# Inverse Fourier products in plain float32 in place of three products of split operands

## Chip, cores and metric

The kernel runs on one core of a Trainium2 chip. Its time is the device time of one execution in microseconds; the median of several executions counts.

## What is computed

One inference step of a two-layer backbone: a Hyena layer (a long convolution by Fourier transforms) and a layer of multi-head latent attention, for 1024 sample tokens and 128 prompt tokens of 1024 channels. The change touches the long convolution of the first layer alone:

```python
def hyena_mix(h, w_in, conv_w, conv_b, ..., f_bias, w_out):
    n = 2 * L
    proj = h @ w_in
    u = short_conv(proj[..., :3 * HY_WIDTH], conv_w, conv_b)
    gate = proj[..., 3 * HY_WIDTH:]
    x0, x1, v = jnp.split(u, 3, axis=-1)
    z = (v * x1).astype(jnp.float32)
    hf = jnp.fft.rfft(filt, n=n, axis=0)
    hf = hf[:, :HY_WIDTH] + jnp.conj(hf[:, HY_WIDTH:])
    y = jnp.fft.irfft(jnp.fft.rfft(z, n=n, axis=1) * hf, n=n, axis=1)[:, :L]
    y = (y + z * f_bias.astype(jnp.float32)).astype(h.dtype) * x0
    return (y * jax.nn.silu(gate)) @ w_out
```

## The kernel before

The channels are worked in eight groups of 128. In the first stage a group's input projections, filter and forward transform are made (`hyena_group`), and the product of spectra goes to DRAM: `PS` for the sample (eight blocks of frequencies, real and imaginary, 128 x 128 each), `PP` for the prompt. The stage that the change touches comes next, from about 600 us on. In it `inverse` (line 532 on) makes y of a group: it loads the spectra in four pairs of blocks (`pi_raw`), multiplies them on TensorE by constant matrices (`ic`, 3200 columns; for the prompt `ip`, 256 columns), evicts the PSUM tile `iv_ps` by ScalarE into `Z` (the first pair) or `W` (the others), line 553, and combines these by 21 operations of VectorE (`ds`, `bf`, `yv`, lines 99 and 102). For five of the groups GpSimd multiplies y by the gate `xg` (`gate_y`, line 99), and y is stored in `YD`, to be loaded again when its place in SBUF is free.

A float32 matrix product is made of three products in float32r, a format that TensorE reads in one go: operand x is split into `hi`, x rounded to float32r, and `lo`, the exact rest, and hi·hi + hi·lo + lo·hi are summed in PSUM. For the spectra ScalarE makes hi (`pi_h`) and GpSimd lo (`pi_l`), for the prompt's (`pp_h`, `pp_l`) ScalarE and VectorE. The constants are split when the stage begins (`load_const`): 13 pieces of 256 columns pass through two buffers `cst`, ScalarE makes hi and VectorE lo.

Beside the inverse transforms TensorE makes the input projections that are left (`in_proj`, line 415: `ip_ps`, 384 columns each, 72 a projection), for x0 and the gate of the last groups; their weights are split by ScalarE and GpSimd (`wi_h`, `wi_l`). The list `PLAN` says how both alternate, `i` being an inverse without `gate_y`. A scheduler orders each engine's instructions when the program is built, and each engine then takes its own in that order; all loads and stores of this stage stand in SP's queue, in order too. Tiles share their places in SBUF: a tile waits until the users of what lay there are done.

Behind the stage `w_out` (line 627, `wo_ps`) needs y of all groups, split again (`lhh`, `lhl`), and then comes the attention layer.

Of the kernel before, what the change touches and what calls it, by code (L numbers as in the profile page):

```python
# [17 lines left out]
P = 128  # L18
D = 1024
# channel groups whose x0 and gate are made along with a group's forward transform  # L20
GATES = (0, None, None, 1, None, None, None, None)
NY = 6          # channel groups inverted before the input projection ends
# [20 lines left out]
# the steps of a unit of attention (scores of the next one, transposes, products with the values)  # L43
# [10 lines left out]
NT = 9          # token tiles: 8 of the sample, 1 of the prompt  # L54
# [15 lines left out]
# columns of the per-partition vector table  # L70
NK = 1408       # keys: 1024 of the sample, 256 of the cache, 128 of the prompt
# [4 lines left out]
class K:  # L76
# [8 lines left out]
    # hi = x rounded to float32r, lo = the exact rest  # L85
# [18 lines left out]
    # ---------------------------------------------------------------- adaLN  # L104
    def ada_chunk(self, layer, o, n, pool, ps, kk, bufs):
        """n columns from o of silu(cond) @ ada_w, as four partial sums on rows 32g + cond."""
# [12 lines left out]
    def ada_col(self, layer, m, o, n, pool, ps, kk, bufs):  # L119
        """columns o.. of shift and scale with the channel on the partition."""  # L120
        self.ada_turn(layer, m, o, n, self.ada_chunk(layer, o, n, pool, ps, kk, bufs), ps)
# [10 lines left out]
    def ada_mod(self, layer, m, A, k):  # L132
        """A = norm_w (1 + scale) for the channel tiles k."""
        c = C_NORM + 8 * layer
        nw = self.cols[:, c + k.start:c + k.stop].unsqueeze(2).broadcast_to([P, k.stop - k.start, 2])
        self.stt(A[:, k], m[:, 8 + k.start:8 + k.stop, :], 1.0, nw, ALU.mult, ALU.add)

    def ada_row(self, layer, gd, o, n, pool, ps, kk, bufs):
        """columns o.. of the gates as rows in DRAM."""
# [13 lines left out]
    # ------------------------------------------------- RMSNorm and modulate  # L153
# [11 lines left out]
    def norm(self, xs, ys, pool, eng=None):  # L165
        """ys = rmsnorm(xs) without its weight; the squares pass through ys, or a tile of their own."""
# [17 lines left out]
    def norm_mod(self, xs, tiles, pool, ps, A, B, hT, lT):  # L184
        """h^T (hi, lo): [128 channels, 8, tokens] of rmsnorm(x) * A + B, for neighbouring token tiles."""
# [12 lines left out]
    def modulate(self, x, k, c, pool, A, B):  # L198
        """x^T A + B for the channels k of the third c of the tokens."""
# [10 lines left out]
    # ------------------------------------------------------------- filters  # L210
    def sin_layer(self, pool, ps, w, src, kk, out, col):
        """out = sin(freq * (w^T src + b)) with the argument reduced to [-pi, pi]."""
# [14 lines left out]
    def load_w3(self, pool, g, bufs):  # L227
        """the last filter weights of 128 channels, forward and backward, on both halves of the rows."""
# [6 lines left out]
    def filters(self, pool, ps, hs):  # L235
        """hs: hidden features [hi; lo] by token."""
# [16 lines left out]
    # -------------------------------------------------------- long convolution  # L253
    def group_filter(self, g, q):
        """time-domain filter of 128 channels into the filter columns of E and O, and of the prompt."""
# [10 lines left out]
        # forward and backward taps: the sample at 0, the prompt at 1025, a zero behind each  # L266
# [9 lines left out]
        # the taps over the sums of their absolute values  # L276
# [11 lines left out]
        # sum and difference of the forward taps and the reversed backward ones  # L288
# [55 lines left out]
    def dft_tile(self, k0, ab, q):  # L344
        """the frequencies k0 + 16 m of z (columns 0:128) and of the filter (128:256)."""
# [22 lines left out]
    def product(self, pt, special, q, out):  # L368
        """out [128, 2, 128] = z * filter; special: row 0 holds two real frequencies."""
# [18 lines left out]
    # ------------------------------------------------------------ Hyena: in  # L388
# [15 lines left out]
    def in_proj(self, m, q, cb):  # L404
        """128 output channels of h @ hy_w_in; cb(psum, token offset)."""
# [16 lines left out]
    def conv_in(self, m, q):  # L422
        """one of x0, x1, v: projection, then the short convolution; [128, 1153] with column 1024 unused."""
        q["last"] = self.in_proj(m, q, lambda pt, o: self.conv_cb(pt, o, q))
        return self.conv(m, q)
# [19 lines left out]
    def hyena_group(self, g, q):  # L445
# [21 lines left out]
        # sample  # L467
# [7 lines left out]
        # prompt  # L475
# [54 lines left out]
    # ----------------------------------------------------------- Hyena: out  # L530
    def inverse(self, g, q):
        """y = irfft(product): [128 channels, T]."""
        nc, pool, ps = self.nc, q["pool"], q["ps"]
        ih, il, jh, jl = q["ih"], q["il"], q["jh"], q["jl"]
        # blocks 1 2 3 7 6 5 of (real, imaginary), and the blocks 0 (even, odd) and 4
        W = pool.tile([P, 6, 2, P], F32, name="W", bufs=1)
        Z = pool.tile([P, 2, 2, P], F32, name="Z", bufs=1)
        for ks, dst in (((0, 4), Z), ((1, 7), W[:, 0:4:3]), ((2, 6), W[:, 1:5:3]), ((3, 5), W[:, 2:6:3])):
            pt = ps.tile([P, 2, 256], F32, name="iv_ps", tag="iv_ps", bufs=3)
            raw = pool.tile([P, 2, 2, P], F32, name="pi_raw", bufs=4)  # L540
            h = pool.tile([P, 2, 2, P], F32R, name="pi_h", bufs=3)
            l = pool.tile([P, 2, 2, P], F32R, name="pi_l", bufs=3)
            st = ks[1] - ks[0]
            nc.sync.dma_start(raw, q["PS"][g][:, ks[0]:ks[1] + 1:st])
            self.hi("act", h, raw)
            self.lo("pool", l, raw, h)
            for b, k0 in enumerate(ks):
                for ri in range(2):
                    o = 256 * ri if k0 == 0 else 512 + 384 * (k0 - 1) + P * (1 - ri)
                    for s, (x, w) in enumerate(((h, ih), (h, il), (l, ih))):  # L550
                        self.PE.matmul(pt[:, b, :], x[:, b, ri, :], w[:, o:o + 256],
                                       start=ri == 0 and s == 0, stop=ri == 1 and s == 2)
# [5 lines left out]
        # d: W1 - W7, W2 - W6, W3 - W5 in blocks 0, 2, 4 (imaginary: 1, 3, 5), s: the sums in blocks 6..11  # L558
# [10 lines left out]
        # a0 a3 a2 a1 in blocks 0..3  # L569
# [22 lines left out]
        # prompt  # L592
        pt = ps.tile([P, 2, 256], F32, name="iv_ps", tag="iv_ps", bufs=3)
        raw, h, l = (pool.tile([P, 2, P], t, name=n, bufs=1) for n, t in (("pp_raw", F32), ("pp_h", F32R), ("pp_l", F32R)))
        nc.sync.dma_start(raw, q["PP"][g])
        self.hi("act", h, raw)
        self.lo("dve", l, raw, h)
        for ri in range(2):
            for s_, (x, wt) in enumerate(((h, jh), (h, jl), (l, jh))):
                self.PE.matmul(pt[:, 0, 0:P], x[:, ri, :], wt[:, P * ri:P * ri + P],  # L600
                               start=ri == 0 and s_ == 0, stop=ri == 1 and s_ == 2)
# [8 lines left out]
    def load_w(self, src, pool, ncol, tag, bufs, raw_bufs=2, hi_eng="act", lo_eng="dve", lo_bufs=None, step=2, tag_raw="w_raw", size=None, stage=None):  # L610
        """a [128, kt, ncol] weight chunk, split."""
# [17 lines left out]
    # ------------------------------------------------------------------ run  # L629
# [25 lines left out]
    def hyena(self):  # L655
# [9 lines left out]
        # in thirds of the tokens: the first ones' place comes free before the last product ends  # L665
# [12 lines left out]
        with self.pool("hsp", side="right") as hp:  # L678
            hs = hp.tile([P, T], F32R, name="hs")
            q.update(hs=hs)  # L680
            with self.pool("fp", 2, side="right") as fp, self.pool("ap", side="right") as ap, \
# [6 lines left out]
                # the normed tokens with the channel on the partition: in places of the convolution's and of x  # L688
# [14 lines left out]
                # the first two projections, along the channels as they come  # L703
# [5 lines left out]
                # shift and scale of 256 channels at a time; a chunk is turned after the next one's products  # L709
# [28 lines left out]
            with self.pool("pf", side="right") as fpool, self.pool("pa", 2, side="right") as pool, \  # L738
                    self.pool("pas", space=PSUM) as ps:
                # what only the filters need lies first: its place is the first to come free  # L740
# [22 lines left out]
        # the constants take the place of what only the filters needed  # L763
        with self.pool("pc", side="right") as pc, self.pool("pb1", 1, side="right") as pool, \
                self.pool("pb1s", space=PSUM) as ps:
            with self.urgent():
                ih, il = self.load_const(pc, "ic", 512 + 7 * 384, pc, "cst", 256, nc.sync)
                jh, jl = self.load_const(pool, "ip", 256, pc, "cst", 256, nc.sync)
            q.update(pool=pool, ps=ps, ih=ih, il=il, jh=jh, jl=jl)
# [15 lines left out]
        # once more in place of the constants: the weights of w_out and y  # L785
# [711 lines left out]
```

## Time and profile before

| | |
|---|---|
| median of 3 executions | 1869.53 us (1867.89 to 1870.08) |
| profiled execution | span 1868.4 us; its own time beside the span isn't recorded |
| TensorE busy | 1785.4 us (96%), 11480 matmuls |
| VectorE busy | 1291.5 us (69%) |
| ScalarE busy | 1116.4 us (60%) |
| GpSimd busy | 616.9 us (33%) |
| chain that ended last | TensorE 51%, VectorE 5%, DMA 2% of the span |

The span runs from the first to the last instruction. In the profile PE is TensorE's matmuls, PEld its loads of weights, DVE VectorE, ACT ScalarE, POOL GpSimd, SP the engine that issues transfers. A matmul's recorded duration contains its way through the array; the pace of a row of matmuls is read from their starts. A plain float32 product is recorded as two matmuls.

### The profile page before, as it was taken

The page shows a single profiled execution, that of the slowest core. Times are in us where ns is not written, and L with a number is a line of the kernel's source. Part 1 is how long each engine was busy: PE and PEld are TensorE (multiplying, and loading weights), DVE is VectorE, ACT ScalarE, POOL GpSimd, SP SyncE. Part 2 cuts the span into 40 slices and gives each one's busy share as a digit, 9 for nine tenths or more (in the row PEclk, how much of TensorE's full clock was granted, in tenths as well). Part 3 has the DMA queues.
Part 4 walks back from the last instruction along what each step waited for, and adds up shares of the span by engine and source line. Part 5 has one row for each costly group of instructions (what it writes and reads, how often), then busy time and mean ns, then how long its engine had stood idle before and what let it go on. Part 6 is the DMA issues. An engine that isn't in the chain of part 4 may idle for free.

```text
span 1868.4 us, 31762 instructions
## 1 busy us (share of the span) xinstructions
PE 1785.4 (96%) x11480; PEld 1585.0 (85%) x11480; DVE 1291.5 (69%) x2556; ACT 1116.4 (60%) x2650; POOL 616.9 (33%) x796
## 2 busy tenths in 40 slices
PE   6998999999999977999999989999999999999998
PEld 4887888887888877788999979999899998998786
DVE  3847887888865699753233268877887888778454
ACT  7655566665653443434353368878887888788431
POOL 2334433344345574233000042424343342235100
PEclk9999999999999988999999989999999999999999
DMA  8222232222223553731313410101010000012541
GB/s 316 83 84 72 66 94 93 82 82 66 74 95 112 168 167 103 279 134 65 94 33 109 102 31 19 42 16 46 20 37 28 20 28 24 18 35 62 180 134 68
DMA packets 126500, 157.93 MB, mean 85 GB/s; under 512 B 12711, under 2 KB 99687, under 8 KB 125064
## 3 DMA queue, kind: packets, MB, share of 16 engines
q1 hardware_dynamic: 123280, 152.51, 25.3%
q10 hardware_dynamic: 2552, 3.39, 0.6%
q8 instruction: 90, 1.47, 0.3%
q14 instruction: 66, 0.54, 0.1%
q0 software_dynamic: 512, 0.02, 0.0%
HBM read 113.89 MB, written 36.73 MB: 81 GB/s over the span
## 4 chain that ended last, share of the span: by engine, by line
PE 51%; DVE 5%; DMA 2%; ACT 1%; SPq 1%; issue 1%; POOL 0%; DVEq 0%; ACTq 0%; POOLq 0%
PE wo_ps L627 18%; PE wo_ps L1289 11%; PE av_ps L1174 8%; PE nm_ps L1162 7%; PE wo_ps L991 4%; PE nm_ps L1023 1%; DVE mx L1292 1%; DVE bf L99 1%; DMA og_in<-og 1%; SPq L978 1%; DMA y<-YD 0%; DVE kT L96 0%; PE nm_ps L842 0%; DMA wm_raw<-wm_a 0%; DVE yv L102 0%
## 5 line engine op out<-in xcount | busy, mean ns | idle before, releaser
L1289 PE MATMUL wo_ps<-kT,qT 128*128 128x512 f32 (+1 forms) x1152 | 281.4, 375 | 11.0 <-POOL qT L90 6.5
L1296 ACT ACTIVATE prob<-wo_ps,mx 128x512 f32<-128x512 f32 (+1 forms) x384 | 234.1, 618 | 22.9 <-DVE mx L1294 20.8
L1292 DVE TENSOR_REDUCE mx<-wo_ps 128x1 f32<-128x512 f32 (+1 forms) x384 | 213.0, 596 | 32.8 <-PE wo_ps L1289 32.1
L88 ACT ACTIVATE pt_h<-nm_ps 128x512 fp32r<-128x512 f32 x324 | 192.8, 599 | 70.4 <-PE nm_ps L1162 62.4
L1289 PEld LDWEIGHTS wo_ps<-kT,qT 128*128 128x128 f32 x1152 | 189.1, 191 | 46.4 <-ACT prob L1296 14.5
L96 DVE TENSOR_TENSOR pt_l<-nm_ps,pt_h 128x512 fp32r<-128x512 f32 x324 | 210.6, 683 | 13.0 <-ACT pt_h L88 12.8
L1162 PE MATMUL nm_ps<-ident,prob 128*128 128x128 f32 x1280 | 191.5, 272 | 0.0
L96 POOL TENSOR_TENSOR wi_l<-wi_raw,wi_h 128x512 fp32r<-128x512 f32 x64 | 127.3, 1989 | 185.1 <-ACT wi_h L88 181.7
L1162 PEld LDWEIGHTS nm_ps<-ident,prob 128*128 128x128 f32 x1280 | 150.0, 140 | 8.5
L415 PE MATMUL ip_ps<-lT,wi_h 128*128 128x384 f32 x720 | 157.1, 346 | 0.0
L415 PE MATMUL ip_ps<-hT,wi_l 128*128 128x384 f32 x720 | 152.8, 344 | 0.0
L415 PE MATMUL ip_ps<-hT,wi_h 128*128 128x384 f32 x720 | 152.5, 346 | 0.0
L1174 PE MATMUL av_ps<-pt_h,Vt 128*128 128x256 f32 x640 | 138.1, 297 | 0.0
L1174 PE MATMUL av_ps<-pt_l,Vt 128*128 128x256 f32 x640 | 135.4, 293 | 0.4 <-DVE pt_l L96 0.4
L415 PEld LDWEIGHTS ip_ps<-lT,wi_h 128*128 128x128 f32 x720 | 128.3, 192 | 6.7 <-issue 4.4
L415 PEld LDWEIGHTS ip_ps<-hT,wi_h 128*128 128x128 f32 x720 | 126.0, 190 | 6.4 <-issue 4.4
L415 PEld LDWEIGHTS ip_ps<-hT,wi_l 128*128 128x128 f32 x720 | 125.2, 189 | 7.1 <-issue 4.7
L627 PE MATMUL wo_ps<-wm_h,lhh 128*128 128x256 f32 (+1 forms) x432 | 126.5, 296 | 2.3 <-ACT wm_h L88 2.2
L1186 POOL TENSOR_SCALAR gt<-gt,sm 128x64 f32<-128x64 f32 x128 | 54.9, 443 | 220.6 <-DVE sm L1177 219.3
L627 PE MATMUL wo_ps<-wm_l,lhh 128*128 128x256 f32 (+1 forms) x432 | 127.1, 295 | 0.0
L627 PE MATMUL wo_ps<-wm_h,lhl 128*128 128x256 f32 (+1 forms) x432 | 126.7, 295 | 0.0
L99 POOL TENSOR_TENSOR pr<-ev 128x256 f32<-128x256 f32 x72 | 79.2, 1102 | 129.9 <-ACT ev L372 78.7
(354 smaller groups left out, 4348.2 us busy)
## 6 DMA issues: line engine op xcount, KB each, us to landing
wi_raw<-w_in SPq DMA_DIRECT2D x64, 256.0 KB, 3.0
ada_w<-ada_w SPq DMA_DIRECT2D x64, 256.0 KB, 2.8
x_in<-xs SPq DMA_DIRECT2D x16, 512.0 KB, 5.3
ada_w<-ada_w SPq DMA_DIRECT2D x8, 1024.0 KB
PS<-pr_o SPq DMA_DIRECT2D x64, 128.0 KB, 2.5
pi_raw<-PS SPq DMA_DIRECT2D x32, 256.0 KB, 3.6
YD<-yv SPq DMA_DIRECT2D x8, 576.0 KB, 4.5
y<-YD SPq DMA_DIRECT2D x8, 576.0 KB
```

The lines of the kernel that those rows point to most:

```text
L88: self.S.activation(out, src, AF.Copy)
L96: e.tensor_tensor(out, src, hi.bitcast(F32), ALU.subtract)
L99: (eng or self.V).tensor_tensor(out, x, y, op)
L415: mm = self.PE.matmul(pt, w[:, k, :], x[c][:, k, :], start=s == 0 and k == 0, stop=s == 2 and k == 7)
L627: self.PE.matmul(pt, x[k][:, sl], w[:, k, :], start=s == 0 and k == 0, stop=s == 2 and k == kt - 1)
L991: self.PE.matmul(pt[:, :n], x[:, k, o:o + P], y[:, k, c], start=s == 0 and k == 0, stop=s == 2 and k == kt - 1)
L1162: self.PE.transpose(pt[:, P * i:P * i + P], u["p"][i % 2][n // 2][:, P * (2 * (n % 2) + i // 2):P * (2 * (n % 2) + i // 2) + P], self.ident)
L1174: self.PE.matmul(u["po"][:, :256], m["V"][:, 2 * n + e, j, :], u[n][1 + s][:, 256 * e:256 * e + 256], start=n == first and e + s == 0, sto ...
L1186: self.G.tensor_scalar(o, o, u["sm"][:, i, 3:4], None, ALU.mult)
L1289: self.PE.matmul(pt[:, :n], x[:, j, P * i:P * i + P], y[:, j, o:o + n], start=s == 0, stop=s == 2)
L1292: self.V.tensor_reduce(mx[:, b:b + 1], c["s", i, b][:, :n], AX.X, ALU.max)
L1296: self.S.activation(c["p"][i][b], c["s", i, b][:, :n], AF.Exp, bias=c["mx"][i][:, 3:4], accum_out=c["sm"][:, i, b:b + 1])
```

## The change

The splits of the inverse transforms' operands go. The constants are loaded as they are, `ic` in two pieces and `ip` in one; spectra and constants are multiplied as float32. `W`, `Z` and `pp_raw` get second buffers. In `inverse`:

```diff
-        ih, il, jh, jl = q["ih"], q["il"], q["jh"], q["jl"]
-        W = pool.tile([P, 6, 2, P], F32, name="W", bufs=1)
-        Z = pool.tile([P, 2, 2, P], F32, name="Z", bufs=1)
+        ic, ip = q["ic"], q["ip"]
+        W = pool.tile([P, 6, 2, P], F32, name="W", bufs=2)
+        Z = pool.tile([P, 2, 2, P], F32, name="Z", bufs=2)
...
             raw = pool.tile([P, 2, 2, P], F32, name="pi_raw", bufs=4)
-            h = pool.tile([P, 2, 2, P], F32R, name="pi_h", bufs=3)
-            l = pool.tile([P, 2, 2, P], F32R, name="pi_l", bufs=3)
...
-            self.hi("act", h, raw)
-            self.lo("pool", l, raw, h)
...
-                    for s, (x, w) in enumerate(((h, ih), (h, il), (l, ih))):
-                        self.PE.matmul(pt[:, b, :], x[:, b, ri, :], w[:, o:o + 256],
-                                       start=ri == 0 and s == 0, stop=ri == 1 and s == 2)
+                    self.PE.matmul(pt[:, b, :], raw[:, b, ri, :], ic[:, o:o + 256], start=ri == 0, stop=ri == 1)
...
-        raw, h, l = (pool.tile([P, 2, P], t, name=n, bufs=1) for n, t in (("pp_raw", F32), ("pp_h", F32R), ("pp_l", F32R)))
+        raw = pool.tile([P, 2, P], F32, name="pp_raw", bufs=2)
         nc.sync.dma_start(raw, q["PP"][g])
-        self.hi("act", h, raw)
-        self.lo("dve", l, raw, h)
...
-            for s_, (x, wt) in enumerate(((h, jh), (h, jl), (l, jh))):
-                self.PE.matmul(pt[:, 0, 0:P], x[:, ri, :], wt[:, P * ri:P * ri + P],
-                               start=ri == 0 and s_ == 0, stop=ri == 1 and s_ == 2)
+            self.PE.matmul(pt[:, 0, 0:P], raw[:, ri, :], ip[:, P * ri:P * ri + P], start=ri == 0, stop=ri == 1)
```

and where the stage begins:

```diff
-                ih, il = self.load_const(pc, "ic", 512 + 7 * 384, pc, "cst", 256, nc.sync)
-                jh, jl = self.load_const(pool, "ip", 256, pc, "cst", 256, nc.sync)
+                ic = pc.tile([P, 512 + 7 * 384], F32, name="ic", bufs=1)
+                nc.sync.dma_start(ic[:, 0:1664], a["ic"][:, 0:1664])
+                nc.sync.dma_start(ic[:, 1664:], a["ic"][:, 1664:])
+                ip = pc.tile([P, 256], F32, name="ip", bufs=1)
+                nc.sync.dma_start(ip, a["ip"])
```

The scheduler makes another order of the stage; before and behind it the order is the same. On TensorE, where the inverse products begin, before (iv_ps are the inverse products, ip_ps the projections; rows are equal instructions in a row):

```order
L415 MATMUL ip_ps<-hT_121,wi_h 128x384 x7
L551 MATMUL iv_ps<-ic_h,pi_h 128x256
L551 MATMUL iv_ps<-ic_l,pi_h 128x256
L415 MATMUL ip_ps<-hT_121,wi_h 128x384
L415 MATMUL ip_ps<-lT_122,wi_h 128x384 x5
L551 MATMUL iv_ps<-ic_h,pi_l 128x256
L551 MATMUL iv_ps<-ic_h,pi_h 128x256
L551 MATMUL iv_ps<-ic_l,pi_h 128x256
L551 MATMUL iv_ps<-ic_h,pi_l 128x256
L415 MATMUL ip_ps<-lT_122,wi_h 128x384 x3
L415 MATMUL ip_ps<-hT_121,wi_l 128x384 x4
```

and now (line 546 is the inverse product of the sample, 591 that of the prompt):

```order
L415 MATMUL ip_ps<-hT_121,wi_l 128x384 x8
L415 MATMUL ip_ps<-hT_123,wi_h 128x384 x3
L546 MATMUL iv_ps<-ic,pi_raw 128x256 x12
L415 MATMUL ip_ps<-hT_123,wi_h 128x384 x5
L415 MATMUL ip_ps<-lT_124,wi_h 128x384
L546 MATMUL iv_ps<-ic,pi_raw 128x256 x4
L591 MATMUL iv_ps<-ip,pp_raw 128x128 x2
L415 MATMUL ip_ps<-lT_124,wi_h 128x384 x5
L546 MATMUL iv_ps<-ic,pi_raw 128x256 x4
L415 MATMUL ip_ps<-lT_124,wi_h 128x384 x2
L415 MATMUL ip_ps<-hT_123,wi_l 128x384 x6
L546 MATMUL iv_ps<-ic,pi_raw 128x256 x12
```

The inverse products begin 20 projections later (108 behind the last product of adaLN, 88 before) and stand closer: 112 projections among them in place of 231, and 221 behind them in place of 122. On GpSimd, in the middle of the stage, before:

```order
L99 TENSOR_TENSOR yv<-yv,xg 128x1152
L96 TENSOR_TENSOR pi_l<-pi_raw,pi_h 128x512 x5
L99 TENSOR_TENSOR yv<-yv,xg 128x1152
L96 TENSOR_TENSOR pi_l<-pi_raw,pi_h 128x512 x3
L96 TENSOR_TENSOR wi_l<-wi_raw,wi_h 128x512
L99 TENSOR_TENSOR yv<-yv,xg 128x1152
L96 TENSOR_TENSOR pi_l<-pi_raw,pi_h 128x512 x2
```

and now, from the second weights of a projection to the end of the stage:

```order
L96 TENSOR_TENSOR wi_l<-wi_raw,wi_h 128x512 x3
L99 TENSOR_TENSOR yv<-yv,xg 128x1152 x2
L99 TENSOR_TENSOR cv<-cv 128x1024
L99 TENSOR_TENSOR cv<-cv 128x128
L96 TENSOR_TENSOR wi_l<-wi_raw,wi_h 128x512
L99 TENSOR_TENSOR yv<-yv,xg 128x1152
L96 TENSOR_TENSOR wi_l<-wi_raw,wi_h 128x512
L99 TENSOR_TENSOR yv<-yv,xg 128x1152 x2
L96 TENSOR_TENSOR wi_l<-wi_raw,wi_h 128x512 x4
```

The 32 splits of spectra are gone; the gate products of y, one of x0 with its gate (`cv`) and the weights' splits are left.

## Rows read from the trace of the kernel before

**Rows 1.** The page, part 2: busy tenths in 40 slices of 46.7 us

```profile
PE   6998999999999977999999989999999999999998
DVE  3847887888865699753233268877887888778454
```

**Rows 2.** Windows: us, busy PE, PEld, DVE, ACT, POOL, PEclk, DMA share, GB/s

```profile
611.70:763.40 151.70, 126.48 (x787) 122.97 (x786) 135.03 (x200) 58.72 (x123) 79.23 (x46) 0.91 0.46 147
640.00:740.00 100.00, 75.38 (x469) 73.05 (x469) 99.24 (x144) 35.34 (x74) 60.71 (x35) 0.86 0.43 135
```

**Rows 3.** Waits, 600 to 760: us in total, times, longest us

```profile
ACT Z L553 <- DVE bf L99: 32.4, 6, 7.0
PE iv_ps L551 <- ACT Z L553: 13.4, 5, 4.4
```

**Rows 4.** Windows: one group on VectorE without, one with GpSimd at work

```profile
744.96:753.07 8.11, 8.11 (x49) 8.11 (x48) 8.04 (x22) 2.38 (x4) 0.00 (x0) 1.00 0.18 73
719.61:735.55 15.94, 11.32 (x68) 11.12 (x68) 15.87 (x25) 5.42 (x11) 8.10 (x6) 0.89 0.21 75
```

**Rows 5.** Timeline of VectorE: start, us, engine, line, operation, count

```profile
725.67 1.84 DVE L99 TENSOR_TENSOR yv<-bf,ds 128x256 f32<-128x256 f32 x2
...
734.12 1.43 DVE L99 TENSOR_TENSOR cv<-cv 128x1024 f32<-128x1024 f32 x2
...
748.36 0.76 DVE L99 TENSOR_TENSOR yv<-bf,ds 128x256 f32<-128x256 f32 x2
```

**Rows 6.** Timeline of GpSimd beside the first of them

```profile
725.57 1.32 POOL L96 TENSOR_TENSOR wi_l<-wi_raw,wi_h 128x512 fp32r<-128x512 f32 x1 [0.17 <-ACT wi_h L88]
```

**Rows 7.** Groups, 600 to 760: busy us, mean ns | idle before, releaser

```profile
L96 POOL TENSOR_TENSOR pi_l<-pi_raw,pi_h 128x512 fp32r<-128x512 f32 x32 | 46.1, 1456 | 16.0 <-ACT pi_h L88 11.2 <-PE iv_ps L600 2.5 <-DMA pi_raw<-PS 2.1
...
L96 DVE TENSOR_TENSOR ic_l<-cst,ic_h 128x256 fp32r<-128x256 f32 x12 | 8.2, 698 | 15.8 <-ACT ic_h L88 15.8
...
L96 DVE TENSOR_TENSOR pp_l<-pp_raw,pp_h 128x256 fp32r<-128x256 f32 x8 | 5.5, 690 | 0.0
```

**Rows 8.** Line 99 on GpSimd, 600 to 760: ns min/median/max, first and last start

```profile
L99 POOL TENSOR_TENSOR yv<-yv,xg x5: 2619/2690/7564, 649.8 to 716.7; 128x1152 f32<-128x1152 f32 x5
L99 POOL TENSOR_TENSOR cv<-cv x4: 457/1424/2391, 598.3 to 632.1; 128x1024 f32<-128x1024 f32 x2, 128x128 f32<-128x128 f32 x2
```

**Rows 9.** Timeline of TensorE

```profile
644.39 0.22 PE L600 MATMUL iv_ps<-ip_h,pp_h 128*128 128x128 f32 x1
...
645.01 0.33 PE L551 MATMUL iv_ps<-ic_h,pi_h 128*128 128x256 f32 x1
...
646.49 2.26 PE L415 MATMUL ip_ps<-hT,wi_l 128*128 128x384 f32 x12
648.59 0.28 PE L551 MATMUL iv_ps<-ic_h,pi_h 128*128 128x256 f32 x1
...
649.90 0.28 PE L551 MATMUL iv_ps<-ic_h,pi_l 128*128 128x256 f32 x1
```

**Rows 10.** Windows: the lowest clock of the stage

```profile
670.00:680.00 10.00, 5.43 (x27) 5.10 (x26) 9.93 (x10) 5.20 (x11) 9.66 (x5) 0.58 0.58 185
```

**Rows 11.** Timeline of TensorE, plain float32: the first recorded matmul, then both

```profile
38.13 0.64 PE L215 MATMUL sf_ps<-zt,w 33*64 33x512 f32 x1
38.13 1.07 PE L215 MATMUL sf_ps<-zt,w 33*64 33x512 f32 x2
```

**Rows 12.** SP's queue at the stage's start, and a window with the loads under way

```profile
602.78 0.94 SPq L516 DMA_DIRECT2D cst<-ic  x2
...
608.00:612.00 4.00, 4.00 (x26) 4.00 (x25) 0.44 (x1) 2.79 (x7) 2.75 (x3) 1.00 0.99 324
```

**Rows 13.** Timeline of TensorE at the end of the projections, and a window

```profile
761.97 1.55 PE L415 MATMUL ip_ps<-hT,wi_h 128*128 128x384 f32 x8
764.92 0.50 PE L627 MATMUL wo_ps<-wo_h,lhh 128*128 128x512 f32 x1 [1.40 <-POOL lhh L90]
...
760.00:780.00 20.00, 16.42 (x74) 13.05 (x73) 17.42 (x15) 9.73 (x13) 7.32 (x3) 1.00 1.03 400
```

More of the change, by code (lines that the diff above doesn't have):

```diff
@@ L766, in hyena @@
             with self.urgent():
-                ih, il = self.load_const(pc, "ic", 512 + 7 * 384, pc, "cst", 256, nc.sync)
-                jh, jl = self.load_const(pool, "ip", 256, pc, "cst", 256, nc.sync)
-            q.update(pool=pool, ps=ps, ih=ih, il=il, jh=jh, jl=jl)
+                ic = pc.tile([P, 512 + 7 * 384], F32, name="ic", bufs=1)
[3 more added lines that the diff above has]
+                nc.sync.dma_start(ip, a["ip"])
+            q.update(pool=pool, ps=ps, ic=ic, ip=ip)
             last = q["dft"][LAST] if LAST else q["last"]
```

## Prediction

> **What bounds the kernel now.** I read the page's slices first: TensorE is the busy engine nearly everywhere, but in slices 15 and 16 of 40 (654 to 747 us) it falls to 7 tenths while VectorE stands at 9 [rows 1]. That is the stage of the inverse transforms. Then the windows: from the first inverse product (611.7) to the end of the last input projection (763.4) TensorE is busy 126.5 of 151.7 us at a mean clock of 0.91; in 640 to 740 it is busy 75.4 of 100 while VectorE is busy 99.2 [rows 2]. Then the waits: ScalarE waits 32.4 us for VectorE before it may evict into Z, and TensorE waits 13.4 us for such evictions [rows 3]. So in this stage VectorE is the bound, and TensorE waits behind it through ScalarE.
>
> Why is VectorE slow there? A whole group of 128 channels takes it 8.11 us when GpSimd does nothing, and 15.94 us when GpSimd is busy 8.10 us [rows 4]. The pair of operations on 128x256 that takes 0.76 us alone takes 1.84 us [rows 5] when it runs beside one GpSimd operation of 1.32 us [rows 6]. Of the 15.94 us, 1.43 us are a gate product of another group [rows 5], and the split of the prompt's spectrum would take some 0.4 us alone (half of a 0.76 us pair). So 15.94 - 8.11 - 1.43 - 0.4 = 6.0 us were lost to 8.10 us of GpSimd work, 0.74 us for each us. On this the page "SBUF — State Buffer" of the Trainium skill (section "SBUF: two separate sides") is harsher: a VectorE operation with two SBUF inputs and a GpSimd operation that reads SBUF exclude each other for the whole instruction, so that a us of GpSimd costs a us; the sum below would then be some 2 us longer, because VectorE has slack there.
>
> **The change, part by part.**
>
> *Removed from the helpers.* GpSimd loses its 32 splits of spectra, 46.1 us; VectorE loses 8.2 us of splits of constants and 5.5 us of the prompt's [rows 7]; ScalarE loses the roundings that go with them. None of these is on TensorE's path by itself, except through VectorE.
>
> *VectorE.* GpSimd keeps five gate products of 2.69 us and a product pair of up to 2.39 + 0.46 us [rows 8], and about four splits of weights of 1.32 us [rows 6]: 13.5 + 2.9 + 5.3 = 21.7 us. So the eight groups should take VectorE 8 x 8.11 + 0.74 x 21.7 = 81 us, 10.1 a group.
>
> *TensorE, the products.* Before: 384 products of 256 columns, one every 0.119 us (11 steps from 648.59 to 649.90), 48 of the prompt every 0.103 us (six from 644.39 to 645.01), and projections of 384 columns every 0.174 us (twelve from 646.49 to 648.59) [rows 9]. In the built order 231 projections stand among the inverse products and 122 behind them. Work at full pace: 384 x 0.119 + 48 x 0.103 + 353 x 0.174 = 45.7 + 4.9 + 61.4 = 112.0 us. The stretch took 151.7, so 39.7 us are lost: 25.2 idle, the rest at the lower clock (0.58 in 670 to 680, [rows 10]) and in the gaps it leaves.
>
> After: 128 plain products. The trace has no plain float32 product with 128x128 weights and 256 columns, but it has some of the filter's first layer: each is two recorded matmuls, and the second one of 512 columns adds 1.07 - 0.64 = 0.43 us to the first [rows 11]. So a pass of 256 columns costs at least 0.215 us. From above: if the weights of each pass (a 128-column product needs 0.11 us, most of it for weights) were not loaded under the pass ahead, 0.325 us. I take 0.22: [rows 11] are the nearest kind, and their 0.43 us is just twice 512 columns at 2.4 GHz, 0.213 us, with nothing left for the second weights. A product is then 0.44 us against 3 x 0.119 = 0.357: 128 x 0.083 = 10.6 us more (9.3 to 37.5 at the ends). The prompt's 16 products, two passes of 0.11: 3.5 us against 4.9. Work after: 112.0 + 10.6 - 1.4 = 121.2 us.
>
> The page "FP8 and Floating Point Precision" of the Trainium skill (section "TensorE Precision Notes") speaks against the change: it counts four passes for a true float32 product, where three stood. At the measured 0.119 us for each that is 0.476 us a product and 4.6 us more than my sum; the two recorded matmuls at twice the streaming time, 0.43 us, are a little better than four of 0.119, and the trace is followed here.
>
> *What stays lost.* The first inverse product stands 20 projections later in the order (108 behind the last adaLN product in place of 88), so at about 611.9 + 20 x 0.174 = 615.4. Its constants are now one load in two pieces, 1.64 MB, with 0.13 MB for the prompt and the first spectra behind it; at 324 GB/s some 6.3 us, asked for where the first piece is today, at 602.8 [rows 12], so there by 609. The load now also waits for a small store on GpSimd's queue, but the projections up to 615.4 hide another 6 us. TensorE's inverse part is 128 x 0.44 + 3.5 + 112 x 0.174 = 79 us, to 695 if it never waits. VectorE can start its first group in earnest at 615.4 + 16 x 0.44 + 6 x 0.174 = 623.5 and ends at 704.5; its last group can't begin before 694.4, so TensorE is held up little, as W, Z and the prompt's spectrum have two buffers and it may run a group ahead. The pace of both is 10 us a group; for their going out of step I leave 4 us, about one of the waits of today. Behind the inverse part stand 221 projections, 38 us, under which VectorE ends and the y's are stored and loaded again.
>
> *Sum.* The last projection ends at 611.7 + 121.2 + 4 = 736.9 in place of 763.4 [rows 13]: 26.5 us. Of the 3.6 us that TensorE then idles in 760 to 780 [rows 13], the wait for the first y's goes and the last gate's chain stays: 1 us. Everything behind moves up unchanged: its order is the same, and TensorE bounds it. Span 1868.4 - 27.5 = 1840.9 us. The profiled execution is known by its span; the median of the runs, 1869.53, is 1.1 us above it, so I predict **1842.0 us**.
>
> **Rivals.**
> 1. *VectorE stays the bound* (0.16). The second buffers let ScalarE and the loads run ahead, but the stores of y, which wait for GpSimd's gate product, stand on SP's queue ahead of the spectra of the group after next; one gate product took 7.6 us today [rows 8]. At 12 us a group VectorE's last one begins at 623.5 + 7 x 12 = 707.5, TensorE's last 221 projections end at 746, and the time is 1851. For it: VectorE at 99% today. Against: 46 of the stage's GpSimd time are gone.
> 2. *Four passes* (0.10): 0.476 us a product, 121.2 + 4.6, so 1847 us.
> 3. *Weights not hidden* (0.10): 0.325 us a pass, work 112.0 + 37.5 + 2 = 151.5 us, which is all that was lost; 2 us of waits and 1 won behind: 1870 us, no change. For it: only 64 columns of weights hide in [rows 11]. Against: weights of 128 columns hide under 256 columns today [rows 9].
> 4. *Slower: plain float32 runs at the low clock* (0.06). Each pass is 0.43 us: 128 x (0.86 - 0.357) = 64.4 us more, the end is at 611.7 + 175.0 + 2 = 788.7, and the time 1869.5 + 25.3 - 1 = 1894. It decides from a pass of 0.33 us on: (39.7 - 2 - 1 + 1.4) / 128 + 0.357 = 0.655 us for two. For it: the clock does fall in this stage, to 0.58 [rows 10]. Against: there TensorE is busy 5.4 of 10 us, and it will be busier.
> 5. *The helpers' relief is fuller* (0.06): no waits and nothing behind, 1842 - 4 - 3 = 1835.
>
> That the second buffers do nothing is possible, and inside the first rival: they matter only where TensorE is ahead of VectorE.
>
> **How the numbers follow.** The forecast has 0.52. Its own range is 1836 (a pass of 0.215, 1 us of waits) to 1850 (0.235, 8 us). With rivals 1, 2 and 5 it makes 0.84 for faster by over 0.2%, some 3.7 us, about what a measurement of this kernel can tell from no change. Rival 3 falls 0.07 on no change and 0.03 on slower, where rival 4 adds 0.06: slower 0.09. The range that leaves rivals 3 and 4 and little else outside is 1834 to 1861.
>
> **What the profile would show.** Right: no GpSimd operation on spectra; 256 matmul records of the inverse every 0.215 to 0.23 us inside a group; VectorE's group between 8.1 and 11 us; ScalarE's waits for Z and W nearly gone; TensorE busy over 9 tenths and at full clock from 615 to 735; the first w_out product near 738. Wrong: records 0.3 us apart or more; a low clock in this stage; TensorE waiting over 10 us for evictions or spectra; VectorE groups still of 14 us without GpSimd beside them; the constants landing after 616.

## The result, and the profile after

The changed kernel takes 1844.34 us (median of 4 executions, 1841.31 to 1850.43), the kernel before 1869.80 in the same comparison: a ratio of 0.9865, 95% interval 0.9844 to 0.9885. The forecast was 1842.0. The profiled execution is the longest of the four: its own time is 1850.43 us, its span 1848.6.

The page, part 2: the busy tenths in 40 slices, now of 46.2 us; PEclk is the granted clock of TensorE.

```profile
PE   6998999999999999799999899999999999999998
DVE  3847787888876596433143277878787888878464
...
PEclk9999999999999999899999989999999999999999
```

The two slices of 7 tenths [rows 1] have become one, the 17th (739 to 786 us), and it is no longer the stage of the inverse transforms but the place behind it. Windows (us, busy PE, PEld, DVE, ACT, POOL, PEclk, DMA share, GB/s), from the old start of the inverse products to the end of the last projection, and the same 100 us as before:

```profile
611.70:739.50 127.80, 123.28 (x642) 115.79 (x641) 102.67 (x185) 39.82 (x77) 37.06 (x17) 0.97 0.64 217
640.00:740.00 100.00, 95.48 (x500) 90.16 (x499) 84.32 (x152) 31.08 (x61) 31.61 (x14) 0.97 0.65 222
```

TensorE's busy time in 640 to 740 rose from 75.38 to 95.48 us while GpSimd's halved from 60.71 to 31.61 and VectorE's fell from 99.24 to 84.32 [rows 2]. The products themselves, on TensorE's timeline (start, us, engine, line, operation, count):

```profile
615.04 5.34 PE L546 MATMUL iv_ps<-ic,pi_raw 128*128 128x256 f32 x24
620.03 1.23 PE L415 MATMUL ip_ps<-hT,wi_h 128*128 128x384 f32 x5
...
623.00 0.61 PE L591 MATMUL iv_ps<-ip,pp_raw 128*128 128x128 f32 x4
623.36 1.12 PE L415 MATMUL ip_ps<-lT,wi_h 128*128 128x384 f32 x5
624.32 1.89 PE L546 MATMUL iv_ps<-ic,pi_raw 128*128 128x256 f32 x8
625.86 0.70 PE L415 MATMUL ip_ps<-lT,wi_h 128*128 128x384 f32 x2
...
738.14 1.55 PE L415 MATMUL ip_ps<-hT,wi_h 128*128 128x384 f32 x8
739.53 0.39 PE L617 MATMUL wo_ps<-wo_h,lhh 128*128 128x512 f32 x1
```

The first product starts at 615.04. Twenty-four passes hold TensorE for 4.99 us and eight for 1.54; the sixteen more cost 3.45, so a pass is 0.216 us (a short row seems quicker because the projection behind it starts under its end). A product of two passes is 0.431 us. The last projection ends at 739.5 in place of 763.4 [rows 13], and the first product of `w_out` follows without a gap.

Of the waits of before, ScalarE's 32.4 us for VectorE before Z and TensorE's 13.4 for those evictions [rows 3], nothing is left. What TensorE waits for now, 600 to 765 us (us in total, times, longest), is two events:

```profile
PE wo_ps L617 <- POOL lhl L96: 11.7, 1, 11.7
PE iv_ps L546 <- DMA pi_raw<-PS: 4.5, 1, 4.5
```

**The wait for spectra.** SP's queue, TensorE and GpSimd around it:

```profile
654.10 0.32 SPq L589 DMA_DIRECT2D pp_raw<-PP  x1
660.97 0.32 SPq L597 DMA_DIRECT2D xg<-XG  x1
661.38 0.38 SPq L777 DMA_DIRECT2D YD<-yv  x1
662.38 0.33 SPq L399 DMA_DIRECT2D wi_raw<-w_in  x1
662.80 3.26 SPq L542 DMA_DIRECT2D pi_raw<-PS  x4
...
668.75 3.75 PE L546 MATMUL iv_ps<-ic,pi_raw 128*128 128x256 f32 x8 [4.52 <-DMA pi_raw<-PS]
...
658.04 2.90 POOL L99 TENSOR_TENSOR yv<-yv,xg 128x1152 f32<-128x1152 f32 x1 [5.55 <-DMA pp_raw<-PP]
```

SP's queue stands still from 654.4 to 660.97: the load of the next gate `xg` has one buffer and waits until GpSimd's gate product, 658.04 to 660.94, has read it; the store of y waits for the same product. Four loads of spectra stand behind them. TensorE waits 4.5 us, and its next eight passes take 3.75 us in place of 1.89: the granted clock is 0.50 from 670 to 674, the lower of its two levels, and back at 1.00 from 676 on.

**The wait behind the stage.** GpSimd, VectorE and TensorE from 732 us on:

```profile
732.70 3.66 POOL L96 TENSOR_TENSOR lhl<-y,lhh 128x1152 fp32r<-128x1152 f32 x1
741.41 14.60 POOL L96 TENSOR_TENSOR lhl<-y,lhh 128x1152 fp32r<-128x1152 f32 x1 [5.05 <-ACT lhh L88]
...
741.37 1.41 DVE L99 TENSOR_TENSOR cv<-cv 128x1024 f32<-128x1024 f32 x2
742.71 1.41 DVE L99 TENSOR_TENSOR y<-y,cv 128x1024 f32<-128x1024 f32 x2
744.05 7.69 DVE L96 TENSOR_TENSOR lhl<-y,lhh 128x1152 fp32r<-128x1152 f32 x6
751.66 1.88 DVE L96 TENSOR_TENSOR wo_l<-w_raw,wo_h 128x512 fp32r<-128x512 f32 x3
...
756.07 0.80 PE L617 MATMUL wo_ps<-wo_h,lhl 128*128 128x512 f32 x1 [11.71 <-POOL lhl L96]
```

The same GpSimd operation on the same shape took 3.66 us and then 14.60. During the second, VectorE issued 13 operations with two inputs, one behind the other, each at its undisturbed speed; they ended at 753.54 and GpSimd 2.47 us later. That is nearly all that the operation takes elsewhere (2.69 us in run 7), so GpSimd seems to have done its work after VectorE's row. In the kernel before it was VectorE that waited:

```profile
763.98 4.62 DVE L99 TENSOR_TENSOR cv<-cv 128x1024 f32<-128x1024 f32 x2 [0.47 <-ACT cv L500]
...
764.95 6.18 POOL L96 TENSOR_TENSOR lhl<-y,lhh 128x1152 fp32r<-128x1152 f32 x2
```

GpSimd's two splits together took 6.18 us, VectorE's pair beside them 4.62 in place of 1.41, and TensorE waited 1.45 us for the splits.

### The profile page after: what moved, and what is told of

It is laid out like the page before. It is cut to its first block, busy times and chain, and to the rows that moved or that the text cites. A ratio compares the mean times of both kernels' runs of the same rounds, so it can differ in the third digit from the quotient of the medians.

```text
span 1848.6 us, 31322 instructions
## 1 busy us (share of the span) xinstructions
PE 1781.4 (96%) x11336; PEld 1579.3 (85%) x11336; DVE 1246.7 (67%) x2534; ACT 1092.8 (59%) x2596; POOL 575.3 (31%) x764
## 4 chain that ended last, share of the span: by engine, by line
PE 84%; DVE 5%; DMA 3%; POOL 3%; ACT 2%; issue 2%; SPq 1%; DVEq 0%; ACTq 0%; POOLq 0%
PE ip_ps L415 18%; PE wo_ps L617 18%; PE wo_ps L1282 12%; PE av_ps L1167 8%; PE nm_ps L1155 7%; PE wo_ps L984 4%; PE df_ps L364 4%; PE iv_ps L546 3%; PE ada_ps L113 1%; POOL wi_l L96 1%; PE nm_ps L1016 1%; DVE mx L1285 1%; PE sf_ps L273 1%; POOL lhl L96 1%; PE sf_ps L298 1%
## 5 line engine op out<-in xcount | busy, mean ns | idle before, releaser
L96 POOL TENSOR_TENSOR wi_l<-wi_raw,wi_h 128x512 fp32r<-128x512 f32 x64 | 116.2, 1816 | 219.2 <-ACT wi_h L88 219.2
L99 POOL TENSOR_TENSOR pr<-ev 128x256 f32<-128x256 f32 x72 | 84.7, 1179 | 134.3 <-ACT ev L372 83.9
```

The source lines that it names most:

```text
L96: e.tensor_tensor(out, src, hi.bitcast(F32), ALU.subtract)
L99: (eng or self.V).tensor_tensor(out, x, y, op)
```

## Experiments

The theory: the stage was bound by VectorE, which GpSimd's splits slowed, and the gain is their removal, not the second buffers and not the products. First four runs on that.

**1. Single buffers.**

```diff
-        W = pool.tile([P, 6, 2, P], F32, name="W", bufs=2)
-        Z = pool.tile([P, 2, 2, P], F32, name="Z", bufs=2)
+        W = pool.tile([P, 6, 2, P], F32, name="W", bufs=1)
+        Z = pool.tile([P, 2, 2, P], F32, name="Z", bufs=1)
...
-        raw = pool.tile([P, 2, P], F32, name="pp_raw", bufs=2)
+        raw = pool.tile([P, 2, P], F32, name="pp_raw", bufs=1)
```

> The changed kernel with W, Z and pp_raw in one buffer each again. The order of TensorE, VectorE, ScalarE and GpSimd is the same as in the changed kernel; only loads of spectra stand elsewhere in SP's queue. Theory (GpSimd's relief of VectorE is the gain): a group's Z and W are read in the first 4 to 7 us of its 10 to 14 us on VectorE, so ScalarE's next four evictions still find room; 1840 to 1850 us. Rival (the second buffers are the gain): ScalarE waits for Z and W again, 20 us or more of them, and the time goes back to 1857 or more.

Measured: 1850.11 us (six executions: 1839.66, 1841.32, 1849.94, 1850.29, 1850.87, 1853.17), ratio 0.9884 (0.9862 to 0.9906). Just past the upper edge of the theory. ScalarE's wait for Z is back, and TensorE hardly feels it; the largest wait is that behind the stage, again with a split of 14.60 us:

```profile
ACT Z L547 <- DVE bf L99: 19.4, 5, 5.1
...
PE wo_ps L617 <- POOL lhl L96: 11.7, 1, 11.7
PE iv_ps L546 <- DMA pi_raw<-PS: 3.0, 2, 2.6
PE iv_ps L546 <- ACT Z L547: 1.0, 1, 1.0
```

Two times near 1840 and four near 1851 hint that the 11.7 us come in some executions and not in others. With that in the way the run doesn't price the buffers; run 9 does.

**2. The second buffers alone**, in the kernel before.

```diff
-        W = pool.tile([P, 6, 2, P], F32, name="W", bufs=1)
-        Z = pool.tile([P, 2, 2, P], F32, name="Z", bufs=1)
+        W = pool.tile([P, 6, 2, P], F32, name="W", bufs=2)
+        Z = pool.tile([P, 2, 2, P], F32, name="Z", bufs=2)
```

> The kernel before with second buffers of W and Z alone; split products stay. Theory: VectorE, slowed by GpSimd's splits, is the bound, so ScalarE's wait for Z goes but TensorE waits elsewhere: 1863 to 1872 us. Rival (the buffers are the gain): 1845 to 1855.

Measured: 1868.98 us (10 executions), ratio 0.9998 (0.9987 to 1.0008). As the theory said: ScalarE's 32.4 us before Z went, and TensorE waited 16.9 us for GpSimd's `pi_l` instead.

**3. GpSimd's splits alone taken away**, in the kernel before.

```diff
-            l = pool.tile([P, 2, 2, P], F32R, name="pi_l", bufs=3)
...
-            self.lo("pool", l, raw, h)
...
-                    for s, (x, w) in enumerate(((h, ih), (h, il), (l, ih))):
+                    for s, (x, w) in enumerate(((h, ih), (h, il), (h, ih))):
```

> The kernel before without GpSimd's splits of spectra: pi_l isn't made, and the third product multiplies the rounded spectrum once more in its place, so the part of the result that pi_l carries is left out; TensorE's work, ScalarE's roundings, VectorE's own splits of constants and single buffers stay. Theory: relieved of 46 us of GpSimd, VectorE takes 10 to 11 us a group plus 13.7 us of splits, TensorE has 112 us of work: the last projection ends near 735 to 745, time 1839 to 1850 us. Rival (what VectorE and ScalarE lose of their own splits, the buffers or the products is the gain): 1860 or more.

Measured: 1844.38 us (1843.15 to 1846.65), ratio 0.9868 (0.9856 to 0.9881): the whole of the change's gain, with the products, the constants' splits and the single buffers of before. The last projection ends at 735.4, 4 us sooner than in the changed kernel; behind it TensorE then waits 6.5 us for GpSimd's rounding `lhh` of the first y, where the kernel before waited 1.4 [rows 13].

**4. The change with GpSimd's work put back.**

```diff
-            nc.sync.dma_start(raw, q["PS"][g][:, ks[0]:ks[1] + 1:st])
+            nc.sync.dma_start(raw, q["PS"][g][:, ks[0]:ks[1] + 1:st]); l = pool.tile([P, 2, 2, P], F32, name="pi_l", bufs=3); self.tt(l, raw, raw, ALU.subtract, self.G)
```

> The changed kernel, in which GpSimd still makes 32 operations of 128x512 on the spectra (the difference of a spectrum with itself, read by nobody). TensorE's order is the same. Theory: VectorE is slowed as before, 8 x 8.11 + 0.74 x 68 = 115 us from 623.5 on, to 739; TensorE's inverse part ends near 725 and 221 projections behind it near 763: 1862 to 1874 us. Rival (GpSimd's work costs nothing): 1841 to 1851 as the changed kernel.

Measured: 1871.00 us (10 executions), ratio 1.0001 (0.9988 to 1.0013). The whole gain is gone. The group on GpSimd (busy us, mean ns of one | idle before):

```profile
L99 POOL TENSOR_TENSOR pi_l<-pi_raw 128x512 f32<-128x512 f32 x32 | 43.5, 1376 | 26.2 <-DMA pi_raw<-PS 26.0
```

and the 115 us that the theory gave VectorE's groups, from 623 on, with 109.97 of them busy:

```profile
623.00:738.00 115.00, 96.10 (x465) 86.30 (x464) 109.97 (x170) 27.08 (x55) 63.03 (x40) 0.94 0.44 146
```

From the first operation on W, at 625.6, to the last at 735.7 the groups took 110.1 us, a little less than the theory's 115. The last projection ends at 761.6, so 22.1 of the 23.9 us that the change won in the stage (763.4 to 739.5) are lost; the rest of this run's time holds the wait behind the stage too, again 11.7 us in the profiled execution. TensorE waits above all for spectra, 13.7 us: in SP's queue the stores of y wait 28.4 us for GpSimd's gate products and 23.0 us for VectorE, and only 2.4 us of waiting is for the added operations to free the spectra's buffers. Nobody reads what these operations write. Runs 3 and 4 settle the first question from both sides.

**5 and 6. The wait behind the stage.** `YP` names the groups whose `lhl` GpSimd makes; run 5 takes both from it, run 6 only the second (`(0,)` in place of `()`).

```diff
-YP, YG = (0, 1), (0, 1, 2, 3, 4)
+YP, YG = (), (0, 1, 2, 3, 4)
```

> The changed kernel with the splits lhl of the first two groups on VectorE in place of GpSimd. Theory (GpSimd's second split, 14.6 us where the same took 3.66 a little earlier, finds no turn while VectorE issues operation after operation, and TensorE waits 11.7 us for it): the wait goes, VectorE has 2.7 us more, so 1835 to 1842 us and single runs within 4 us of each other, where the changed kernel's are 9 us apart. Rival (the y's and VectorE's own chain are what is late): TensorE waits 6 us or more for a split of VectorE instead, 1843 to 1850.

> The same for the second of the two splits alone; the first stays on GpSimd, where it took 3.66 us and was made before it was wanted. Theory: 1835 to 1842 us, within 4 us. Rival: 1843 to 1850.

Measured: 1839.30 us (1835.66 to 1840.10), ratio 0.9836 (0.9822 to 0.9850), and 1839.04 (1834.88 to 1841.21), 0.9833 (0.9818 to 0.9849). TensorE's wait is down to 1.3 and 2.1 us, on VectorE's `lhl`. The spread is 4.4 us and 6.3, both more than the 4 that were expected, so this wait isn't all that made the changed kernel's times differ.

**7. Spectra a group further ahead.**

```diff
-            raw = pool.tile([P, 2, 2, P], F32, name="pi_raw", bufs=4)
+            raw = pool.tile([P, 2, 2, P], F32, name="pi_raw", bufs=8)
```

> The changed kernel with eight buffers of spectra (pi_raw) in place of four: in SP's queue each group's spectra stand a group further ahead, in front of the gates and stores that wait for GpSimd's gate product. VectorE's and GpSimd's order is the same. Theory (the loads stuck behind that wait cost TensorE 4.5 us idle and 2 to 3 us at a lower clock): the last projection ends at 731 to 736 in place of 739.5; the swings of the wait for GpSimd's split behind it stay, so single runs from 1833 to 1845, median 1835 to 1842. Rival (VectorE is the bound, TensorE only waits elsewhere): no wait for spectra but as much for evictions, the last projection at 738 or later, 1842 to 1850.

Measured: 1840.02 us (1838.47 to 1841.96), ratio 0.9844 (0.9831 to 0.9858). The time is within the theory's range, but not for its reason. No wait for spectra was left, TensorE was busy 40.00 of 40 us from 640 to 680 at full clock, and yet the last projection ended at 739.5 as before. Two waits ahead of it took back what was won, on TensorE's timeline:

```profile
721.35 0.96 PE L415 MATMUL ip_ps<-hT,wi_h 128*128 128x384 f32 x4 [1.61 <-ACT u L430]
725.92 1.65 PE L415 MATMUL ip_ps<-hT,wi_h 128*128 128x384 f32 x4 [3.61 <-ACT wi_h L88]
```

and SP's queue ahead of the second:

```profile
713.93 0.33 SPq L777 DMA_DIRECT2D YD<-yv  x1
...
718.58 0.38 SPq L399 DMA_DIRECT2D wi_raw<-w_in  x1
```

The last weights are asked for at 718.58, behind the store of the last y, which SP's queue issues at 713.93 when VectorE has made it. In this execution GpSimd's second `lhl` took 2.69 us, and VectorE's operation beside it 3.91 in place of 1.41: this time VectorE waited. It is this, and not the loads ahead, that kept the time down in the profiled execution: its span is 8.4 us shorter than the changed kernel's with the projections ended at the same time.

**8. Runs 5 and 7 together.**

```diff
-YP, YG = (0, 1), (0, 1, 2, 3, 4)
+YP, YG = (), (0, 1, 2, 3, 4)
...
-            raw = pool.tile([P, 2, 2, P], F32, name="pi_raw", bufs=4)
+            raw = pool.tile([P, 2, 2, P], F32, name="pi_raw", bufs=8)
```

> Both: eight buffers of spectra, and the first two groups' lhl on VectorE. Theory: the two gains add, 1829 to 1837 us. Rival: with the projections ended sooner, y of the last groups or VectorE's chain at the end of the stage is late, and less than half of the second gain is left: 1838 to 1844.

Measured: 1837.57 us (1836.29 to 1841.85), ratio 0.9835 (0.9820 to 0.9850). Above the theory's range (1829 to 1837): the two don't add, as TensorE's 3.6 us for the last weights stay.

**9. Run 5 with single buffers**: the edits of runs 1 and 5 in one.

```diff
-YP, YG = (0, 1), (0, 1, 2, 3, 4)
+YP, YG = (), (0, 1, 2, 3, 4)
...
-        W = pool.tile([P, 6, 2, P], F32, name="W", bufs=2)
-        Z = pool.tile([P, 2, 2, P], F32, name="Z", bufs=2)
+        W = pool.tile([P, 6, 2, P], F32, name="W", bufs=1)
+        Z = pool.tile([P, 2, 2, P], F32, name="Z", bufs=1)
...
-        raw = pool.tile([P, 2, P], F32, name="pp_raw", bufs=2)
+        raw = pool.tile([P, 2, P], F32, name="pp_raw", bufs=1)
```

> The changed kernel with lhl of the first two groups on VectorE, and W, Z and pp_raw in one buffer each, to be read beside the same with two buffers (1839.3 us): without the swings of GpSimd's split. Theory (the second buffers bring little, as VectorE and not ScalarE's evictions set the pace): ScalarE waits 15 to 25 us for VectorE before Z again, but the time is 1837 to 1843 us. Rival (they are part of the gain): 1845 or more.

Measured: 1838.55 us (1835.69 to 1839.81), ratio 0.9837 (0.9816 to 0.9859), beside 1839.30 with two: the second buffers are worth nothing here.

**10. Another kind of work on GpSimd.**

```diff
-            nc.sync.dma_start(raw, q["PS"][g][:, ks[0]:ks[1] + 1:st])
+            nc.sync.dma_start(raw, q["PS"][g][:, ks[0]:ks[1] + 1:st]); l = pool.tile([P, 2, 2, P], F32, name="pi_l", bufs=3); [self.G.tensor_scalar(l, raw, 1.0, 0.0, ALU.mult, ALU.add) for _ in range(3)]
```

> The changed kernel, in which GpSimd copies each block of spectra three times (one input, 128x512, read by nobody): about 45 us of GpSimd work like the dummy differences' 43.5, but with one input in place of two. If any GpSimd operation on SBUF holds VectorE up: 1862 to 1874 us, as with the differences. If only operations with two inputs do: 1841 to 1851, as the changed kernel, and pairs of VectorE operations on 128x256 beside these copies take 0.76 us.

Measured: 1873.98 us (10 executions), ratio 1.0027 (1.0014 to 1.0039). Copies hold VectorE up too (the 96 took 77.8 us, not the 45 that I had worked out). The time alone doesn't show it, because the copies read the spectra's buffers and the loads of spectra wait 26.1 us in SP's queue for them; the pace of both engines beside each other does:

```profile
645.88 1.57 DVE L99 TENSOR_TENSOR yv<-bf,ds 128x256 f32<-128x256 f32 x2
647.38 1.57 DVE L102 SCALAR_TENSOR_TENSOR bf<-ds 128x256 f32<-128x256 f32 x2
648.88 1.57 DVE L102 SCALAR_TENSOR_TENSOR yv<-bf 128x256 f32<-128x256 f32 x2
...
641.86 9.82 POOL L542 TENSOR_SCALAR pi_l<-pi_raw 128x512 f32<-128x512 f32 x12
```

GpSimd makes a copy every 0.82 us (9.82 / 12) and VectorE an operation every 0.75, by the starts; a pair takes 1.57 us, where alone it takes 0.76 [rows 5]: as if the two took turns.

**11. All five gate products on VectorE too**, in the kernel of run 8 (`YG` names the groups whose y GpSimd multiplies by the gate).

```diff
-YP, YG = (), (0, 1, 2, 3, 4)
+YP, YG = (), ()
```

> Eight buffers of spectra, the first two groups' lhl and all five gate products of y on VectorE. VectorE has 5 x 1.34 us more of its own and is held up 5 x 2.8 us of GpSimd less. Theory (TensorE is already full from 640 to 720 with eight buffers, and behind it waits for weights): no more than 2 us to either side of 1837.6. Rival (VectorE still sets the pace of the stage): 1834 or less.

Measured: 1831.75 us (1828.68 to 1833.41), ratio 0.9801 (0.9779 to 0.9823). The theory was wrong by 6 us. Against run 8, VectorE ends its groups at 705.7 in place of 714.7, so the last y is stored at 705.68 in place of 714.67, the last weights are asked for at 710.73 in place of 719.40, and TensorE isn't idle once before 732. Of each of these differences 2.0 us came from ahead of the stage, as the first inverse product starts at 614.00 and in run 8 at 615.98. The window from the old start to the end of the last projection:

```profile
611.70:730.80 119.10, 119.10 (x637) 112.47 (x636) 99.08 (x192) 39.02 (x76) 16.89 (x11) 1.00 0.67 232
```

In run 8 VectorE no longer bounded TensorE by evictions, but still did by SP's queue. This is the best version.

**12. Run 11 with four buffers of spectra.**

```diff
-            raw = pool.tile([P, 2, 2, P], F32, name="pi_raw", bufs=8)
+            raw = pool.tile([P, 2, 2, P], F32, name="pi_raw", bufs=4)
```

> The changed kernel with lhl of the first two groups and the five gate products of y on VectorE, spectra in four buffers as in the change. TensorE's order is that of the kernel with lhl alone moved (1839.3 us). Theory (in front of the spectra SP's queue then waits for VectorE's gate product, 1.34 us, in place of GpSimd's, 2.9 us, and VectorE's groups are 1 us shorter): the wait for spectra falls from 4.8 us to 2 or less, 1833 to 1837 us. Rival (the eight buffers were what made the 1831.75 us): the wait stays over 4 us, 1838 or more.

Measured: 1836.63 us (1831.87 to 1838.78), ratio 0.9822 (0.9800 to 0.9844). As the theory had it: the wait for spectra is 1.5 us. From the first inverse product to the end of the last projection this kernel takes 118.6 us and run 11's 116.8, so the spectra loaded ahead are worth 1.8 us there. The medians are 4.9 us apart, but the two intervals overlap, and the rest of that isn't explained.

## Why the prediction was right, and where not

- **The bound and its cause**: right. Runs 3 and 4 show that GpSimd's 32 splits were nearly the whole of it: the last projection ends at 735.4 without them in the old kernel, in place of 763.4, and at 761.6 with as much GpSimd work in the new, in place of 739.5.
- **The products**: right. 0.216 us a pass beside 0.22; the weights hide under the pass ahead and nothing fell to the low clock for being float32, so rivals 3 and 4 fall. Rival 2 falls too: 0.431 us a product, not 0.476.

The rule on the four passes of true float32, in the Trainium skill ("FP8 and Floating Point Precision", section "TensorE Precision Notes"), can't be counted here, as the records show two matmuls a product, but the measured time agrees with it. If a pass takes a column in each cycle of 2.4 GHz, four passes of 256 columns are an estimated 0.427 us, beside 0.431 measured: what was too dear in rival 2 was 0.119 us for a pass.

- **The start**: 615.04 us beside 615.4; the constants were no hindrance.
- **VectorE**: 81 us for the eight groups, 10.1 a group, was too little: from the first operation on W, at 624.5, to the last at 711.9 they took 87.4. Windows of three groups, each from its first operation to the next group's:

```profile
643.81:657.97 14.16, 14.16 (x73) 12.97 (x72) 14.00 (x21) 3.78 (x9) 7.86 (x4) 1.00 0.78 254
658.01:669.90 11.89, 7.37 (x36) 6.44 (x35) 11.72 (x21) 3.41 (x7) 4.31 (x2) 0.92 0.67 218
669.94:680.80 10.86, 10.86 (x44) 9.67 (x43) 10.65 (x22) 2.34 (x4) 2.87 (x1) 0.77 0.55 186
```

The first two are longer than the 8.1 to 11 us that the prediction named as a sign of being right. Above the 8.11 us of an undisturbed group [rows 4] the three lose 12.58 us to 15.04 us of GpSimd, 0.84 for each, not 0.74. Over the whole stretch the forecast's price holds: of the 87.4 us, 64.9 are eight undisturbed groups and 2.8 are two operations on `cv` that the sum left out; the other 19.7 stand beside 26.8 us of GpSimd, 0.73 for each. So it was GpSimd's time that was too small, 21.7 us: beside VectorE its operations are recorded longer, up to 4.78 us for a split of weights put at 1.32.

The Trainium skill's rule ("SBUF — State Buffer", section "SBUF: two separate sides"), that a GpSimd operation that reads SBUF and a VectorE operation with two SBUF inputs exclude each other for the whole instruction, was read in the prediction as a us for a us. Both prices here, 0.84 and 0.73, lie below that; but GpSimd's records can contain its own waits for VectorE, as the 14.60 us above do, so they don't contradict the rule.

- **What stays lost in the stage**: mis-sized. Four us were left for waits. TensorE's own work is seen in run 11, without a gap and at full clock: 116.8 us from the first inverse product to the end of the last projection, and with the 3.3 us ahead of it (611.7 to 615.04) 120.1, not 121.2. The stretch took 127.8, so 7.7 us were lost: 4.5 idle and some 3 at the lower clock behind it. The mechanism is that of rival 1, loads of spectra behind a gate product of GpSimd in SP's queue, at about half the price that it had there. The two errors leave the last projection at 739.5 beside 736.9.
- **The step that failed** is "the wait for the first y's goes and the last gate's chain stays: 1 us". The chain of splits behind the stage was already a race of VectorE and GpSimd, which VectorE lost in the kernel before (4.62 us for its pair on `cv`) and GpSimd in the changed one: TensorE lost 11.7 us there in the profiled execution. Without that wait (run 5) the median is 1839.3, so the change lost some 5 us of its median there; all nine executions of runs 5 and 6 lie below all four of the changed kernel, and run 9 beside run 1 (1838.55 and 1850.11 us) shows the same more clearly.
- **Behind the stage**: from the first product of the attention's weights, at 874.2 us before and 859.4 after, to the end took 994.2 us before and 989.2 after. In the 14 profiled executions of this case it is from 988.1 to 994.2, whatever was changed. Of the 5 us between these two, 2.5 are TensorE's idle time (27.5 us before, 25.0 after) and the rest is busy time; what makes them wasn't tried.
- **The second buffers**: they do nothing (runs 2 and 9).

So 1842.0 beside 1844.34 is in part luck, from errors of both signs: 2.6 us late at the last projection, 10 more behind it in the profiled execution, and 5 won back in a part that the change doesn't touch. For the profiled execution that is 1840.9 + 2.6 + 10 - 5 = 1848.5, with a span of 1848.6. One slip stands in the prediction's own range: a pass of 0.215 and 1 us of waits make 1842.0 - 1.3 - 3 = 1837.7, not 1836.

## What to carry to other kernels

Work moved to GpSimd isn't free while VectorE is the bound: price it at some 0.7 to 0.85 us of VectorE's time for each recorded us where both read two inputs (0.73 over the stage and 0.84 in three groups here), and expect copies to hold VectorE up too; a dearer product on TensorE that saves such work can pay. Where both engines feed one consumer, don't leave a piece that is wanted early on GpSimd beside a long row of VectorE operations: it may get no turn until the row ends. And when a wait for loads goes, look for what else stands in the same queue behind the late engine: here the last weights waited behind the store of the last y, and of what was tried only taking GpSimd's gate products from beside VectorE freed both.

## What was not expected of the hardware

One GpSimd operation, `lhl` of 128x1152, took 14.60 us in three kernels (the changed one and runs 1 and 4), and 2.69 to 3.87 us wherever else it is recorded by itself. VectorE's 13 operations ran at full speed all through the 14.60; in run 7 it was VectorE that waited. In the three long cases GpSimd's operation starts 0.03 to 0.04 us after the start of one of VectorE's (741.41 beside 741.37), in the 14 others 0.09 us or more after one. That goes with the outcome each time, but no run moved this offset on purpose, so what decides who gets the first turn isn't shown; a profile of one of the quick executions of runs 1 and 4 wasn't taken.
